# Where the sums over an expert's slots stand in TensorE's order: behind the first half of a gate and up group

## The chip, the cores and the metric

The kernel runs on one core of a Trainium2 chip. The metric is the device time of one execution in microseconds (us). TensorE (PE in the profile) multiplies matrices into PSUM, VectorE (DVE) and ScalarE (ACT) move and combine, SyncE (SP) issues the DMA transfers that bring the weights from HBM to SBUF. Each engine works through its own queue of instructions in order; between engines there are semaphores.

## The reference

Two layers of a trunk over 256 tokens of width 1024. Each layer has a token mixer and a channel mixer; the channel mixer of the second layer is a mixture of eight experts of which each token takes two:

```python
def moe_swiglu(x, router, wg, wu, wd):
    ...
    top_val, top_idx = lax.top_k(logits, TOP_K)
    top_w = jax.nn.softmax(top_val, axis=-1)
    gates = jnp.sum(jax.nn.one_hot(top_idx, N_EXPERTS, dtype=jnp.float32) * top_w[..., None], axis=1)
    out = jnp.zeros((B * S, D), jnp.float32)
    for e in range(N_EXPERTS):
        out = out + gates[:, e:e + 1] * swiglu(xt, wg[e], wu[e], wd[e]).astype(jnp.float32)
```

All is float32. An expert's hidden width is 2816, so each of its three weight matrices has 1024 x 2816 elements.

## The kernel before, in words

The change touches the expert stage alone (`moe`, from about 437 us on in the profiled execution). The tokens of an expert are gathered into slots: 64 always (the main slots) and 32 more (the unit slots) when the expert has over 64 tokens, which is known on the chip only; a flag for each expert is read into a register, and a condition on it chooses at run time. Up to 96 slots are thus computed in one round, and further rounds are skipped unless an expert has more tokens.

An expert is worked through in three chunks of its hidden width (1024, 1024 and 768). For each chunk:

- the gate and up group: 32 products for the main slots (L756, `gu<-raw,xg`, 64 rows out) and 32 for the unit slots, over eight tiles `raw` of weights;
- ScalarE and VectorE make the hidden values from `gu` (L879, L880), and TensorE transposes them into `pt` (L889), which VectorE copies to `hT` (L891);
- the down group of the chunk before (`down`, L756, `y<-raw,hT`), which accumulates over an expert's chunks in two PSUM banks: `y[0]` for the main slots and `y[1]` for the unit slots. `y[1]` is opened and closed by a matmul with zeros (`clear`, L763).

Every group is issued by `in_steps`: first the half of the main products that needs no flag (`ahead`, 16 products, two rows each in the trace), then the condition, then in either branch the rest. A product on TensorE stands in two rows of the trace, as it is float32.

After an expert's last down group, `combine` moves `y` to SBUF as a pair of a rounded part `yh` (ScalarE, L838) and the remainder `yl` (VectorE, L839), six pieces each: two of 64x512 (main slots, from `y[0]`) and four of 32x256 (unit slots, from `y[1]`). `add_up` then sums over the slots: for each of four output quarters a PSUM bank `pc` gets one matmul with `yh` (L848) and one with `yl` (L849), and VectorE adds the bank, times the gate, to `x` (L850). The banks `pc` come from a pool of two, which `pt` shares, so the third pair can be written when the first addition has read its bank. `y` too has a pool of two banks, so the next expert's `y[1]` takes a bank that the expert before has used.

The order on an engine is set by a scheduler that takes what is ready by its place in the program, within the dependences; `behind(a, b)` adds a dependence for the order alone. `flush` calls `add_up` behind the second gate and up group of the next expert; the scheduler drew the sums ahead of that group, since no dependence held them.

The weights pass through a ring of 16 tiles of up to 1 MB: SyncE issues the load of a tile (L744) when TensorE has read what was in it.

Of the kernel before, what the change touches and what calls it, by code (L numbers as in the profile page):

```python
# [54 lines left out]
def hybrid_trunk_kernel(ctx, tc, x_in, w_in, pool_w, relx, w_out, lnrow, vecs, ffn_wg, ffn_wu, ffn_wd,  # L55
                        router, moe_wg, moe_wu, moe_wd, ca_in, cb_in, out):
    nc = tc.nc
# [9 lines left out]
    def bank(pool, tag, name):  # L67
        return pool.tile([P, 512], F32, tag=tag, name=name)
# [41 lines left out]
    def behind(inst, first):  # L110

        tc.add_manual_dep(inst.ins, first.ins.name,
                          mybir.DependencyInfo(mybir.DependencyClass.NoSync, mybir.DependencyReason.DATA),
                          reason="order")
# [508 lines left out]
    def moe(i, mp, pss, r):  # L623
# [5 lines left out]
        yh = mp.tile([P, D], F32R, name="yh")  # L629
# [19 lines left out]
        for t in range(NT):  # L649
# [5 lines left out]
            for hf in range(2):  # L655
                c = slice(hf * 512, (hf + 1) * 512)
                ps = bank(mm, "mm", "xn")
# [51 lines left out]
        def gather(e0, base):  # L709

            pm = mp.tile([P, NT, 2, P], F32R, tag="pm", name="pm")
            pT = mp.tile([P, 2, NT, P], F32R, tag="pmT", name="pmT", bufs=2)
            for j in range(2):
                for t in range(NT):

                    last = nc.vector.tensor_scalar(pm[:, t, j, :], slots, float(base - 4096),
                                                   key[:, t, e0 + j:e0 + j + 1], op0=ALU.add, op1=ALU.is_equal)
            if e0 == 0 and base == 0:
                pm_done.append(last)
                low_parts(last)  # L720
                for t, c, ps in starts:
                    behind(nc.scalar.mul(x[:, t, c], ps, ALPHA), norm)

            g = mp.tile([P, KD, 2 * P], F32, tag="xg", name="xg", bufs=2)
            for k in range(0, KD, 2):
                ps = bank(tr, "tr", "pg")
                for kk in range(2):
                    for n, (src, t) in enumerate((s, t) for s in (nh, nl) for t in range(NT)):
                        nc.tensor.matmul(ps[:, kk * 256:(kk + 1) * 256], src[:, t, (k + kk) * P:(k + kk + 1) * P],
                                         pm[:, t, :, :], start=(n == 0), stop=(n == 2 * NT - 1))  # L730
                nc.scalar.activation(g[:, k:k + 2, :], ps.rearrange("p (a n) -> p a n", a=2), AF.Copy)
            for j in range(2):
                ps = bank(tr, "tr", "pq")
                for t in range(NT):
                    nc.tensor.matmul(ps[:, t * P:(t + 1) * P], pm[:, t, j, :], identr, start=True, stop=True)
                nc.scalar.activation(pT[:, j, :, :], ps[:, :S].rearrange("p (t n) -> p t n", t=NT), AF.Copy)
            return g, pT
# [14 lines left out]
        order = [None]  # L752
# [8 lines left out]
        def clear(ps, n=512, first=True, last=True):  # L761

            nc.tensor.matmul(ps[:, :n], zero[:, :P], zero[:, :n], start=first, stop=last)  # L763

        def in_steps(flag, ahead, main, unit, rest):


            order[0] = None
            if flag is None:
                ahead()  # L770
                main()
                unit(0)
                unit(1)
                return
            ahead()
            with tc.If(flag > 0) as has:
                order[0] = None
                unit(0)
                main()
                unit(1)  # L780
            with has.Else():
                order[0] = None
                rest()
                main()
            order[0] = None

        def experts(base):
# [9 lines left out]
            for e in range(NE):  # L797
                if e == 0:
                    g, pT = gather(e, base)
# [12 lines left out]
                def down(f0, n, hT, e=e, y=y, flag=flag):  # L812

                    nj = n // P
                    wd = moe_wd[e][f0:f0 + n, :].rearrange("(p j) d -> p j d", j=nj)
                    if not y:
                        y.extend(bank(yp, "yp", "y") for _ in range(2))
                        clear(y[1], 256, last=False)
                    ws = [pieces(wd[:, j:j + 2, :], D) for j in range(0, nj, 2)]

                    def part(sls, js, own):
                        for j in js:
                            for sl, b, r, c in sls:
                                product(y[b][r:r + sl.stop - sl.start, :c.stop - c.start], hT[:, j, sl],
                                        ws[j // 2][:, j % 2, c], own and f0 == 0 and j == 0,
                                        own and f0 + n == DFF and j == nj - 1)

                    steps = range(4), range(4, nj)
                    main, unit = blocks(D)[:2], blocks(D)[2:]
                    in_steps(flag, lambda: part(main, steps[0], True), lambda: part(main, steps[1], True),  # L830
                             lambda i: part(unit, steps[i], False), lambda: None)
                    if f0 + n == DFF:
                        clear(y[1], 256, first=False)

                def combine(e=e, pT=pT, y=y):
                    for sl, b, r, c in blocks(D):
                        ps = y[b][r:r + sl.stop - sl.start, :c.stop - c.start]
                        last_yh[0] = nc.scalar.activation(yh[sl, c], ps, AF.Copy)  # L838
                        nc.vector.tensor_sub(yl[sl, c], ps, yh[sl, c])  # L839

                    sums.append(lambda: add_up(e, pT))

                def add_up(e, pT):
                    for hf in range(2):
                        c = slice(hf * 512, (hf + 1) * 512)
                        for t in range(NT):
                            ps = bank(tr, "tr", "pc")
                            nc.tensor.matmul(ps, pT[:, e % 2, t, :], yh[:, c], start=True, stop=False)  # L848
                            nc.tensor.matmul(ps, pT[:, e % 2, t, :], yl[:, c], start=False, stop=True)  # L849
                            nc.vector.scalar_tensor_tensor(x[:, t, c], ps, gate[:, t, e:e + 1], x[:, t, c],  # L850
                                                           op0=ALU.mult, op1=ALU.add)

                for ci, (f0, n) in enumerate(ECH):
# [6 lines left out]
                    def part(m, k0, ws=ws, gu=gu, g=g, w=w):  # L860
                        s0 = 0 if m == MAIN else MAIN

                        for k in (k0 + 2, k0 + 3, k0, k0 + 1):
                            for b in range(2):
                                for i in range(2):
                                    bk, r = (b, i * MAIN) if m == MAIN else (2, (2 * i + b) * UNIT)
                                    product(gu[bk][r:r + m, :w], g[:, k, o + s0:o + s0 + m],
                                            ws[k // 2][1 - i][:, k % 2, b * w:(b + 1) * w], k == 2, k == KD - 3)

                    in_steps(flag, lambda: part(MAIN, 0), lambda: part(MAIN, 4), lambda i: part(UNIT, 4 * i),  # L870
                             lambda: clear(gu[2], w))
                    if e % 2 and e + 1 < NE and ci == len(ECH) - 1:
                        nxt = gather(e + 1, base)
                    s = mp.tile([P, 1024], F32, tag="silu", name="silu", bufs=2)
                    for b in range(2):
                        c = slice(b * w, (b + 1) * w)
# [17 lines left out]
                    if ci == len(ECH) - 1:  # L894
                        later.append(combine)
                        if e % 2 and e + 1 < NE:
                            g, pT = nxt
# [13 lines left out]
        for t in range(NT):  # L911
            mu, r = moments(t)
            for hf in range(2):
                c = slice(hf * 512, (hf + 1) * 512)
# [21 lines left out]
    with tc.tile_pool(name="moe", bufs=1) as mp, tc.tile_pool(name="ring2", bufs=RING2) as ring2:  # L936
        rings.append((ring2, RING2))
        ring_pos[0] = 0
        moe(1, mp, pss, r)
# [56 lines left out]
```

## Time and profile before

| | |
|---|---|
| time, three runs | 1170.47, 1172.53, 1173.04 us (median 1172.53) |
| the profiled execution | 1171.37 us, span of its instructions 1169.6 us |
| TensorE busy | 1112.1 us (95% of the span) |
| VectorE, ScalarE busy | 425.3 us, 292.6 us |
| mean granted TensorE clock | 0.965 of full speed |
| DMA, 450 to 1150 us | 264.23 MB, mean 377 GB/s |

The profile lists for each engine what it did and what ended its waits. [...] A row of the timeline merges equal instructions that follow each other: start, duration to the end of the last, engine, line, operation, names, and in brackets the idle time ahead of it and what ended it.

### The profile page before, as it was taken

To read this page: it belongs to the slowest core of one execution; us is meant where nothing else is said; L and a number is where in the kernel's file an instruction comes from. 1 tells how busy PE (TensorE), PEld (TensorE's weight loads), DVE (VectorE), ACT (ScalarE), POOL (GpSimd) and SP (SyncE) were. 2 spreads that over 40 slices of the span, in tenths; PEclk is the share of its full clock that TensorE was granted. 3 is DMA by queue.
4 is the path that set the end of the run, shared out by engine and by line. 5 is a ranking of instruction groups with operands and counts; after the bars stand their busy time and mean duration, and the time that the engine had idled before them with its cause. 6 is when DMAs were issued, how large, how long until landed. Compare 5 with 4: busy or idle time off the path is not lost. (4 is left out here: it accounts for less than half of the span.)

```text
span 1169.6 us, 15303 instructions
## 1 busy us (share of the span) xinstructions
PE 1112.1 (95%) x6494; PEld 616.6 (53%) x6494; DVE 425.3 (36%) x708; ACT 292.6 (25%) x450; POOL 3.2 (0%) x15
## 2 busy tenths in 40 slices
PE   8999999999999999998998998998998998998995
PEld 6987688888789774333433332433333443333333
DVE  3677755453597763113113113113113112113115
ACT  2455454443345643001101001101001101001001
POOL 0000000000000000000000000000000000000000
PEclk9999999999999988998998998999998999998996
DMA  8942385555276259999999899989899989999911
GB/s 252 315 154 72 122 274 180 180 181 172 79 266 225 73 197 415 408 416 415 411 369 416 344 413 414 414 352 413 342 415 414 411 338 415 356 413 418 413 60 38
DMA packets 108766, 350.19 MB, mean 299 GB/s; under 512 B 7680, under 2 KB 31360, under 8 KB 97408
## 3 DMA queue, kind: packets, MB, share of 16 engines
q1 hardware_dynamic: 108528, 348.75, 77.1%
q8 instruction: 73, 1.20, 0.4%
q14 instruction: 21, 0.17, 0.0%
q10 hardware_dynamic: 144, 0.07, 0.0%
HBM read 347.75 MB, written 1.05 MB: 298 GB/s over the span
## 5 line engine op out<-in xcount | busy, mean ns | idle before, releaser
L756 PE MATMUL gu<-raw,xg 128*64 128x512 f32 (+3 forms) x2304 | 401.6, 568 | 0.5 <-issue 0.5
L756 PEld LDWEIGHTS gu<-raw,xg 128*64 128x64 f32 (+1 forms) x2304 | 131.2, 130 | 252.6 <-issue 248.3
L880 DVE TENSOR_TENSOR silu<-silu,gu 64x512 f32<-64x512 f32 (+1 forms) x96 | 61.9, 645 | 432.1 <-ACT silu L879 429.7
L756 PE MATMUL y<-raw,hT 128*64 128x512 f32 (+1 forms) x1408 | 200.9, 489 | 0.0
L879 ACT ACTIVATE silu<-gu 64x512 f32<-64x512 f32 (+1 forms) x96 | 53.1, 553 | 501.6 <-PE gu L756 496.4
L126 DVE TENSOR_TENSOR lo<-raw,hi 128x2048 fp32r<-128x2048 f32 (+1 forms) x57 | 128.0, 2251 | 84.8 <-ACT hi L125 84.8
L125 ACT ACTIVATE hi<-raw 128x2048 fp32r<-128x2048 f32 (+1 forms) x57 | 107.4, 1883 | 135.1 <-PE gu L146 42.1
L756 PEld LDWEIGHTS y<-raw,hT 128*64 128x64 f32 (+1 forms) x1408 | 68.1, 123 | 121.3 <-issue 107.8
L144 PE MATMUL ps<-xTh,hi 128*128 128x256 f32 x224 | 65.2, 291 | 1.2 <-DVE vs L348 0.7
L146 PE MATMUL ps<-xTh,lo 128*128 128x256 f32 x224 | 64.5, 288 | 1.6 <-DVE lo L126 1.6
L144 PE MATMUL gu<-hi,xTh 128*128 128x512 f32 (+1 forms) x176 | 65.9, 374 | 0.0
L145 PE MATMUL gu<-lo,xTh 128*128 128x512 f32 (+1 forms) x176 | 65.7, 373 | 0.0
L146 PE MATMUL gu<-hi,xTl 128*128 128x512 f32 (+1 forms) x176 | 65.5, 372 | 0.0
L145 PE MATMUL ps<-xTl,hi 128*128 128x256 f32 x224 | 64.4, 287 | 0.0
L891 DVE COPY hT<-pt 128x384 f32<-128x384 f32 (+1 forms) x48 | 22.9, 519 | 94.7 <-PE pt L889 94.7
L144 PEld LDWEIGHTS ps<-xTh,hi 128*128 128x128 f32 x224 | 43.5, 194 | 2.5 <-issue 1.0
L146 PEld LDWEIGHTS ps<-xTh,lo 128*128 128x128 f32 x224 | 43.6, 195 | 2.2 <-DVE lo L126 1.8
L145 PEld LDWEIGHTS ps<-xTl,hi 128*128 128x128 f32 x224 | 43.5, 194 | 0.4 <-issue 0.3
L848 PE MATMUL pc<-yh,pmT 128*128 128x512 f32 x32 | 15.8, 586 | 28.4 <-ACT yh L838 28.4
L838 ACT ACTIVATE yh<-y 32x256 fp32r<-32x256 f32 (+1 forms) x48 | 21.5, 447 | 77.9 <-PE y L756 47.9
L145 PEld LDWEIGHTS gu<-lo,xTh 128*128 128x128 f32 x176 | 33.2, 188 | 5.7 <-DVE lo L126 0.3
L146 PEld LDWEIGHTS gu<-hi,xTl 128*128 128x128 f32 x176 | 33.2, 188 | 5.7 <-issue 0.2
(186 smaller groups left out, 1078.8 us busy)
## 6 DMA issues: line engine op xcount, KB each, us to landing
raw<-in_moe_wd_dram SPq DMA_DIRECT2D x88, 1024.0 KB, 13.1
raw<-in_moe_wu_dram SPq DMA_DIRECT2D x64, 1024.0 KB, 14.0
raw<-in_moe_wg_dram SPq DMA_DIRECT2D x64, 1024.0 KB, 15.2
raw<-in_moe_wu_dram SPq DMA_DIRECT2D x32, 768.0 KB, 12.5
raw<-in_moe_wg_dram SPq DMA_DIRECT2D x32, 768.0 KB, 14.2
raw<-in_w_in_dram SPq DMA_DIRECT2D x14, 1024.0 KB, 9.8
raw<-in_ffn_wg_dram SPq DMA_DIRECT2D x11, 1024.0 KB, 5.1
raw<-in_ffn_wu_dram SPq DMA_DIRECT2D x11, 1024.0 KB, 5.0
```

What stands on the lines that cost most here:

```text
L125: cv = nc.scalar.activation(hi[:, :a * n], raw[:, :a * n], AF.Copy)
L126: ld = nc.vector.tensor_sub(lo[:, :a * n], raw[:, :a * n], hi[:, :a * n])
L144: nc.tensor.matmul(o, ah, bh, start=first, stop=False)
L145: nc.tensor.matmul(o, ah, bl, start=False, stop=False)
L146: nc.tensor.matmul(o, al, bh, start=False, stop=last)
L756: mi = nc.tensor.matmul(o, a, b, start=first, stop=last)
L838: last_yh[0] = nc.scalar.activation(yh[sl, c], ps, AF.Copy)
L848: nc.tensor.matmul(ps, pT[:, e % 2, t, :], yh[:, c], start=True, stop=False)
L879: nc.scalar.activation(s[sl, c], gu[bk][rg:rg + m, :w], AF.Silu)
L880: nc.vector.tensor_mul(s[sl, c], s[sl, c], gu[bk][ru:ru + m, :w])
L891: nc.vector.tensor_copy(hT[:, j0:j0 + m, :], pt[:, :m * SLOTS].rearrange("p (j q) -> p j q", q=SLOTS))
```

## The change: what it does

`in_steps` remembers the last product of the half that stands ahead of the condition, and the first matmul of each of the four pairs of `add_up` gets an order dependence on it. So the sums of expert e are issued behind the 16 products `ahead` of the group that was begun last, and in front of that group's condition.

```diff
+        last_ahead = [None]
+
         def in_steps(flag, ahead, main, unit, rest):
             order[0] = None
             if flag is None:
                 ahead()
+                last_ahead[0] = order[0]
                 main()
                 unit(0)
                 unit(1)
                 return
             ahead()
+            last_ahead[0] = order[0]
             with tc.If(flag > 0) as has:
...
                         for t in range(NT):
                             ps = bank(tr, "tr", "pc")
-                            nc.tensor.matmul(ps, pT[:, e % 2, t, :], yh[:, c], start=True, stop=False)
+                            behind(nc.tensor.matmul(ps, pT[:, e % 2, t, :], yh[:, c], start=True, stop=False),
+                                   last_ahead[0])
                             nc.tensor.matmul(ps, pT[:, e % 2, t, :], yl[:, c], start=False, stop=True)
```

On TensorE, where one expert ends and the next has begun, this stood in a row before, from the matmul that closes the old `y[1]` to the first product of the next group (a name in brackets is the semaphore of the engine or DMA queue that the instruction waits for):

```order
L763 MATMUL y<-zero 128x256
L848 MATMUL pc<-yh,pmT 128x512 [waits Activation_49]
L848 MATMUL pc<-yh,pmT 128x512 [waits DVE_49]
L763 LDWEIGHTS zero
L763 MATMUL y<-zero 128x256 [waits DVE_49]
L849 MATMUL pc<-yl,pmT 128x512 [waits DVE_49]
L849 MATMUL pc<-yl,pmT 128x512
L848 MATMUL pc<-yh,pmT 128x512 [waits Activation_49]
L848 MATMUL pc<-yh,pmT 128x512 [waits DVE_49]
L849 MATMUL pc<-yl,pmT 128x512 [waits DVE_49]
L849 MATMUL pc<-yl,pmT 128x512
L756 MATMUL gu<-raw,xg 64x512 [waits DMAHW2_49]
```

And this stands there now, from the matmul that opens the next expert's `y[1]` on; "..." stands for the rest of the 16 products (a line number that is 4 or 5 higher is the same statement):

```order
L763 LDWEIGHTS zero
L763 MATMUL y<-zero 128x256 [waits DVE_49]
L756 MATMUL gu<-raw,xg 64x512 [waits DMAHW2_49,Activation_49]
...
L852 MATMUL pc<-yh,pmT 128x512 [waits PE_49,Activation_49]
L854 MATMUL pc<-yl,pmT 128x512 [waits DVE_49]
L852 MATMUL pc<-yh,pmT 128x512 [waits PE_49]
L854 MATMUL pc<-yl,pmT 128x512
L852 MATMUL pc<-yh,pmT 128x512 [waits DVE_49,Activation_49]
L854 MATMUL pc<-yl,pmT 128x512
L852 MATMUL pc<-yh,pmT 128x512 [waits DVE_49]
L854 MATMUL pc<-yl,pmT 128x512
L780 COMPARE_AND_BRANCH
```

The eight matmuls of the sums have gone from ahead of the 16 products to behind them, directly ahead of the condition; the second matmul with zeros, which opens the next `y[1]` and waits for VectorE, has stayed where it was and now stands directly ahead of the products. The count of VectorE that it waits for is in the built program, in both kernels and at all seven places, that of the third piece of `yl` (the second of 64x512). This holds at the seven changes from one expert to the next; behind the last expert nothing moves.

On VectorE, between the copies of `hT` and the next group's hidden values, this stood before:

```order
L839 TENSOR_TENSOR yl<-y,yh 64x512
L839 TENSOR_TENSOR yl<-y,yh 32x256
L839 TENSOR_TENSOR yl<-y,yh 64x512
L839 TENSOR_TENSOR yl<-y,yh 32x256
L850 SCALAR_TENSOR_TENSOR x<-pc,gate,x 128x512
L839 TENSOR_TENSOR yl<-y,yh 32x256
L850 SCALAR_TENSOR_TENSOR x<-pc,gate,x 128x512
L839 TENSOR_TENSOR yl<-y,yh 32x256
L850 SCALAR_TENSOR_TENSOR x<-pc,gate,x 128x512 x2
```

And now:

```order
L843 TENSOR_TENSOR yl<-y,yh 64x512
L843 TENSOR_TENSOR yl<-y,yh 32x256
L843 TENSOR_TENSOR yl<-y,yh 64x512
L843 TENSOR_TENSOR yl<-y,yh 32x256 x3
L855 SCALAR_TENSOR_TENSOR x<-pc,gate,x 128x512 x4
```

The last two pieces of `yl` no longer stand behind additions that wait for the sums. ScalarE, GpSimd and SyncE have the same order in both kernels.

## Rows read from the trace of the kernel before

**Rows 1.** The page: busy us, share of the span, instructions

```profile
PE 1112.1 (95%) x6494; PEld 616.6 (53%) x6494; DVE 425.3 (36%) x708; ACT 292.6 (25%) x450; POOL 3.2 (0%) x15
```

**Rows 2.** Who waited for whom, 450 to 1150 us: total us, times, longest

```profile
PE pc L848 <- ACT yh L838: 27.0, 15, 2.3
...
PEld gu L756 <- DMA raw<-in_moe_wd_dram: 2.1, 5, 0.7
```

**Rows 3.** What the DMA queue of SyncE waited for, 450 to 1150 us

```profile
SPq L744 <- PE gu L756: 168.6, 45, 13.6
```

**Rows 4.** DMA, 450 to 1150 us: GB/s in 40 slices, total

```profile
GB/s 419 402 416 419 409 420 406 362 397 413 415 294 415 413 418 413 416 374 347 412 415 292 413 418 411 418 409 415 285 410 422 317 412 414 411 424 402 417 14 1
DMA packets 61460, 264.23 MB, mean 377 GB/s; under 512 B 4287, under 2 KB 4287, under 8 KB 50135
```

**Rows 5.** Timeline of TensorE at the first change of expert, 528 to 552 us

```profile
534.44 0.28 PE L763 MATMUL y<-zero 1*128 1x256 bf16 x1
536.92 0.74 PE L848 MATMUL pc<-yh,pmT 128*128 128x512 f32 x2 [2.20 <-ACT yh L838]
537.59 0.39 PE L763 MATMUL y<-zero 1*128 1x256 bf16 x1
537.91 1.22 PE L849 MATMUL pc<-yl,pmT 128*128 128x512 f32 x2
540.41 1.22 PE L848 MATMUL pc<-yh,pmT 128*128 128x512 f32 x2 [1.28 <-ACT yh L838]
541.43 1.05 PE L849 MATMUL pc<-yl,pmT 128*128 128x512 f32 x2
542.41 9.88 PE L756 MATMUL gu<-raw,xg 128*64 128x512 f32 x48
```

**Rows 6.** Timeline of VectorE at the same place

```profile
536.50 1.14 DVE L839 TENSOR_TENSOR yl<-y,yh 64x512 fp32r<-64x512 f32 x2 [0.21 <-ACT yh L838]
538.74 0.75 DVE L850 SCALAR_TENSOR_TENSOR x<-pc,gate,x 128x512 f32<-128x512 f32 x1 [1.10 <-PE pc L849]
539.52 0.42 DVE L839 TENSOR_TENSOR yl<-y,yh 32x256 fp32r<-32x256 f32 x1
```

**Rows 7.** Timeline of ScalarE at the same place

```profile
535.87 0.99 ACT L838 ACTIVATE yh<-y 64x512 fp32r<-64x512 f32 x2 [0.74 <-DVE yl L839]
```

**Rows 8.** Groups by line and form, 450 to 1150 us: busy us, mean ns

```profile
L850 DVE SCALAR_TENSOR_TENSOR x<-pc,gate,x 128x512 f32<-128x512 f32 x32 | 23.3, 748 | 14.4 <-PE pc L849 14.2
...
L839 DVE TENSOR_TENSOR yl<-y,yh 64x512 fp32r<-64x512 f32 x16 | 11.0, 688 | 17.7 <-ACT yh L838 17.5
```

**Rows 9.** Stretches of 2 us there: length, busy PE, PEld, DVE, ACT, POOL, clock, DMA

```profile
535.00:537.00 2.00, 0.08 (x1) 0.08 (x1) 1.72 (x4) 1.10 (x3) 0.00 (x0) 1.00 1.01 408
537.00:539.00 2.00, 2.00 (x5) 0.81 (x5) 0.87 (x3) 0.38 (x1) 0.00 (x0) 0.63 1.03 424
...
543.00:545.00 2.00, 2.00 (x8) 0.60 (x6) 0.50 (x1) 0.00 (x0) 0.00 (x0) 0.67 1.03 430
```

**Rows 10.** Stretches, seven changes of expert: first matmul with zeros ended, `ahead` ended

```profile
534.72:550.43 15.71, 12.23 (x46) 4.50 (x49) 6.38 (x11) 2.09 (x5) 0.00 (x0) 0.78 1.02 424
...
1066.05:1082.13 16.08, 12.42 (x45) 4.42 (x49) 6.37 (x11) 2.09 (x5) 0.00 (x0) 0.79 1.02 422
sum 110.87, PE 86.20 PEld 31.01 DVE 44.60 ACT 14.64 POOL 0.00; mean PE 12.31 PEld 4.43 DVE 6.37 ACT 2.09 POOL 0.00
```

**Rows 11.** Timeline of TensorE in expert 0: 16 products in a row

```profile
455.68 7.09 PE L756 MATMUL gu<-raw,xg 128*64 128x512 f32 x32
```

**Rows 12.** Stretches of 1 us early in the program, columns as in rows 9

```profile
37.00:38.00 1.00, 0.00 (x0) 0.00 (x0) 1.00 (x1) 1.00 (x1) 0.00 (x0) 1.00 1.09 386
...
39.00:40.00 1.00, 1.00 (x7) 1.00 (x7) 0.94 (x3) 0.55 (x1) 0.00 (x0) 0.58 1.01 344
...
42.00:43.00 1.00, 1.00 (x8) 1.00 (x8) 1.00 (x1) 0.21 (x1) 0.00 (x0) 0.71 1.05 375
```

**Rows 13.** TensorE's sequencer at the conditions: ns min/median/max, first and last start

```profile
L776 PEldq COMPARE_BRANCH  x72: 65/174/1977, 450.1 to 1143.7; - x72
```

## The prediction

> **What bounds the kernel now.** I read the page first: TensorE is busy for 1112.1 us of a span of 1169.6 us [rows 1]. Then who waited for whom in the expert stage. TensorE itself waits for almost nothing there but ScalarE's `yh` ahead of the sums, 27.0 us in 15 waits; for the weights only its weight loads wait, and the longest such total is 2.1 us in 5 waits [rows 2]. The transfers, on the other side, wait for TensorE to free tiles of the ring: 168.6 us at its gate and up products alone [rows 3]. At their best they run at some 415 GB/s, over the stage at 377 [rows 4], so 264.23 MB need at least 264.23 / 0.415 = 637 us of 700, and there are 63 us of slack. So TensorE is the bound, and time saved on it at a change of expert should reach the end.
>
> The timeline of TensorE at one change of expert shows what is to be had [rows 5]. The first matmul with zeros ends at 534.72. TensorE is idle for 2.20 us until `yh` is there, does two matmuls of the sums, opens the next `y[1]`, does two more, is idle for another 1.28 us, does the last four, and begins the 16 products at 542.41. The second idle stretch comes from VectorE's order: a piece of `yl` starts only at 539.52, behind an addition that had waited for the sums [rows 6].
>
> The clock is the second thing to see. It is at the upper level in the first idle stretch, and 0.63 on the mean from 537 to 539, so it fell at 537 + 2 x (1 - 0.37 / 0.5) = 537.5; 0.67 from 543 to 545 puts its rise at 544.3 [rows 9]. That is 6.8 us at the lower level, with an idle stretch inside it and the 16 products only at its end. All seven changes look alike: 15.71 to 16.08 us from the end of the first matmul with zeros to the end of the 16 products, 110.87 us in all (15.84 each), and a mean clock of 0.78 or 0.79, which over 15.8 us is 6.6 to 7.0 us at the lower level [rows 10].
>
> **The change part by part.** No instruction is added and none taken away; the eight matmuls of the sums move behind the 16 products at seven places. I rebuild the same interval with the new order.
>
> 1. The wait that stays. The matmul that opens the next `y[1]` now stands ahead of the products, and TensorE takes its matmuls in order. It needs the third piece of `yl`: VectorE starts that at 536.50 [rows 6] and takes 0.69 us [rows 8], so 537.19. From ScalarE's end at 535.87 + 0.99 = 536.86 [rows 7] to the matmul that it released at 536.92 [rows 5] it is 0.06 us; the same here gives 537.25. TensorE is thus idle for 537.25 - 534.72 = 2.53 us, where it was idle for 2.20. Nothing on VectorE or ScalarE ahead of that piece moves, so I take it as fixed.
> 2. The matmul with zeros, to the start of what follows: 537.59 to 537.91, 0.3 us [rows 5].
> 3. The 16 products: 7.09 us at the upper level [rows 11]. Their weights were landed long before; beginning them some 5 us earlier needs no transfer that TensorE waits for in the rows.
> 4. The lower level. The wait of 2.53 us is longer than the one behind which the clock fell seven times, so I let it fall again. How long it stays low is nowhere shown for this order, so I bound it: nothing if it does not fall; 6.8 us as now; or what an early place shows. There TensorE was idle (busy 0.00 from 37 to 38), the clock was 0.58 on the mean of 39 to 40 and 0.71 of 42 to 43, so it was low from 39.16 to 42.58, 3.4 us, with TensorE busy without a break [rows 12]. Behind the wait there now stand 7 us of products without a break, so I take this row: 3.4 us at half speed cost 1.7 us. The ends are 0 and 3.4 us.
> 5. The sums, at the upper level. The pairs `yh`, `yl` for the third and fourth bank wait for the first and second addition, as there are two banks. At the upper level the first two matmuls start 0.34 us apart (0.67 us to the next row for two [rows 5]). From the start of a `yl` matmul to its addition it is 0.83 us at the lower level (537.91 to 538.74 [rows 5, 6]), about 0.5 at the upper; two additions take 2 x 0.75 [rows 8]; the last pair starts 0.06 later and takes 2 x 0.34. So 0.34 + 0.5 + 1.5 + 0.06 + 0.68 = 3.1 us at most. The other end is eight matmuls at half of the 0.51 us between their starts at the lower level (541.43 - 540.41 for two [rows 5]), 2.0 us. The chain of additions is the nearer, but part of the 0.68 is generous: 2.8 us. All of `yh` and `yl` is ready long before, behind 7 us of products, and so costs nothing; without that cover it would be the 1.28 us of now.
> 6. The condition now stands behind matmuls that wait, with only the last pair in TensorE's queue to cover it. Its median is 0.17 us [rows 13], inside the 0.34 us of one matmul: nothing, up to 1.98 - 0.34 = 1.6 us at its longest.
>
> The interval becomes 2.53 + 0.3 + 7.09 + 1.7 + 2.8 = 14.4 us, 1.4 less than 15.84; seven times, 9.9 us. What follows is unchanged in order. VectorE's additions come later, but nothing reads `x` before the end, and the banks that they free are next wanted by transposes behind a whole group. SyncE gets the tiles of the 16 products back earlier, which helps the transfers. Behind the last expert nothing changes.
>
> The profiled execution took 1171.37 us around its span of 1169.6, so 1161.5; the median of the three runs is 1.16 us above it, so I predict 1162.6 us.
>
> [...]
>
> **The rivals.**
>
> - The lower level lasts as long as now. For it: seven of seven stretches were 6.8 us. Against it: in each of them there was an idle stretch of 1.28 us or more inside, which is gone, and the early row is 3.4 us. Price: 1.7 us more at each place, 16.1 us against 15.84, so 2.0 us slower than before, 1174.5; with the sums at 3.1 us, 4.1 slower, 1176.6. It decides where item 4 costs over 3.1 us. Slower or no change.
> - The condition is exposed at its longest each time: 7 x 1.6 = 11.5 us, so 1174.1, slower by 1.6. It decides from 1.4 us each. The median of 0.17 speaks against it, and where the expert has unit slots the code goes straight on.
> - The clock does not fall, or falls late, since the work behind the wait is dense: 7 x 1.7 = 12 us less, 1150.6. Against it: seven falls of seven behind a shorter wait.
> - The transfers take back half, because TensorE gains on them in a stretch: 1167.5. For it: weight loads did wait 2.1 us in 5 places [rows 2], and slices with gaps lie beside full ones at 415 GB/s [rows 4]. Against it: 63 us of slack, and tiles freed earlier.
>
> **How the numbers follow.** Chances: the forecast 0.63; the clock's stretch as long as now 0.13 (0.08 of it within 0.2% and 0.05 slower); the condition 0.04; no fall 0.10; the transfers 0.08; 0.02 for something else that is slower. A measurement of this kernel tells about 0.2% (2.3 us) from no change. Faster: 0.63 + 0.10 + 0.08 = 0.81, taken as 0.80; within 0.2%: 0.08 and most of the condition's, 0.12; slower: 0.08. The forecast's own range is 1157 to 1167: the sums at 2.0 us give 5.6 us more, at 3.1 us 2.1 less, and a place or two with a long stretch 1.7 each. The range for 8 in 10 leaves out the rival without a fall (0.10) and the slower ones beyond the nearest (0.08): 1155 to 1175.
>
> **What would show it.** Per step: an idle stretch of about 2.5 us ahead of the second matmul with zeros, released by VectorE's `yl`; the 16 products directly behind it, in 8.8 us instead of 7.09; a low clock of 3.4 us at each of seven places; then eight matmuls of the sums in 2 to 3.1 us with a short wait for additions; a mean interval near 14.4 us; a mean clock of the run some 0.01 higher than 0.965. Wrong would be: a clock at 0.50 for nearly 7 us into the products, a gap between the sums and what follows the condition, waits of TensorE for weights above the few us of now, or no idle stretch ahead of the products.

## The result, and the profile after

The change makes the kernel faster: 1159.89 us (median of four runs, 1159.42 to 1160.76) against 1172.78 us (four runs of the kernel before beside them, 1170.47 to 1173.22), a ratio of 0.9895 with an interval of 0.9881 to 0.9909. The profiled execution took 1159.93 us, its span is 1158.1 us, the mean granted clock 0.973 instead of 0.965.

The page, busy time of the engines and the clock in 40 slices ("answers [rows 1]" means: the same view as there, now of the changed kernel or of the one under test):

```profile
PE 1105.2 (95%) x6494; PEld 612.8 (53%) x6494; DVE 424.6 (37%) x708; ACT 292.3 (25%) x450; POOL 3.2 (0%) x15
...
PEclk9999999999999988999999999999999999999996
```

TensorE is busy for 6.9 us less, with the same 6494 instructions: the same matmuls at a higher clock, 0.973 on the mean against 0.965. At the seven changes of expert, whose stretches follow below, it is 86.20 - 80.29 = 5.9 us of busy time less; the other 3.7 us saved there are idle time.

The timeline of TensorE at the first change of expert (answers [rows 5]):

```profile
532.52 0.28 PE L763 MATMUL y<-zero 1*128 1x256 bf16 x1
535.32 0.26 PE L763 MATMUL y<-zero 1*128 1x256 bf16 x1 [2.52 <-DVE yl L843]
535.51 8.78 PE L756 MATMUL gu<-raw,xg 128*64 128x512 f32 x32
544.22 0.51 PE L852 MATMUL pc<-yh,pmT 128*128 128x512 f32 x1
544.57 0.40 PE L854 MATMUL pc<-yl,pmT 128*128 128x512 f32 x1
...
545.90 0.47 PE L852 MATMUL pc<-yh,pmT 128*128 128x512 f32 x1 [0.47 <-DVE x L855]
...
546.47 0.51 PE L852 MATMUL pc<-yh,pmT 128*128 128x512 f32 x1
546.81 0.40 PE L854 MATMUL pc<-yl,pmT 128*128 128x512 f32 x1
547.14 5.08 PE L756 MATMUL gu<-raw,xg 128*32 128x512 f32 x38
```

The first idle stretch has grown from 2.20 to 2.52 us, and its releaser is another one: VectorE's `yl`, for which the opening of the next `y[1]` waits. The second idle stretch, 1.28 us, is gone; 0.47 us of waiting for an addition is what the sums have of their own. Behind the last `yl` matmul the unit products follow at once, so the condition between them shows no gap.

The timeline of VectorE there (answers [rows 6]):

```profile
533.23 1.13 DVE L843 TENSOR_TENSOR yl<-y,yh 64x512 fp32r<-64x512 f32 x2
534.57 1.14 DVE L843 TENSOR_TENSOR yl<-y,yh 64x512 fp32r<-64x512 f32 x2 [0.21 <-ACT yh L842]
...
545.00 1.41 DVE L855 SCALAR_TENSOR_TENSOR x<-pc,gate,x 128x512 f32<-128x512 f32 x2 [7.56 <-PE pc L854]
546.65 1.41 DVE L855 SCALAR_TENSOR_TENSOR x<-pc,gate,x 128x512 f32<-128x512 f32 x2 [0.23 <-PE pc L854]
```

In its second row, a piece of 64x512 and one of 32x256 in one, lies the third piece of `yl`; TensorE's wait ends at 535.32, as that piece ends. The additions now start 7.56 us behind the last piece of `yl`, and nothing waits for them but the third pair of the sums.

The seven intervals from the end of the first matmul with zeros to the end of the later of `ahead` and the sums, so over the same work as [rows 10]:

```profile
532.80:547.21 14.41, 11.43 (x45) 3.93 (x48) 5.43 (x10) 2.09 (x5) 0.00 (x0) 0.88 1.03 425
630.69:646.09 15.40, 12.40 (x42) 4.15 (x41) 5.43 (x10) 2.09 (x5) 0.00 (x0) 0.78 0.84 334
...
sum 101.24, PE 80.29 PEld 27.66 DVE 37.98 ACT 14.61 POOL 0.00; mean PE 11.47 PEld 3.95 DVE 5.43 ACT 2.09 POOL 0.00
```

101.24 against 110.87 us are 9.6 us saved at the seven places. Six of them take 14.20 to 14.41 us at a clock of 0.88; the second takes 15.40 at 0.78. The clock in stretches of 2 us at the first and at the second change (answers [rows 9]):

```profile
535.00:537.00 2.00, 1.68 (x7) 0.58 (x8) 1.10 (x3) 0.75 (x2) 0.00 (x0) 0.84 1.02 420
537.00:539.00 2.00, 2.00 (x6) 0.48 (x4) 0.43 (x1) 0.00 (x0) 0.00 (x0) 0.50 1.04 428
539.00:541.00 2.00, 2.00 (x10) 0.67 (x8) 0.00 (x0) 0.00 (x0) 0.00 (x0) 0.81 1.03 420
...
631.00:633.00 2.00, 0.00 (x0) 0.00 (x0) 1.73 (x4) 1.12 (x3) 0.00 (x0) 0.73 0.98 406
...
637.00:639.00 2.00, 2.00 (x8) 0.64 (x6) 0.00 (x0) 0.00 (x0) 0.00 (x0) 0.56 1.03 402
```

Read as in the prediction: 0.84 puts the fall at 537 - 2 x (1 - 0.84) / 0.5 = 536.36, 0.81 the rise at 539.76, so 3.4 us at the lower level, the 0.50 that the stretch between them shows. It is the level of the kernel before too, in a stretch that lies wholly between the fall at 537.5 and the rise at 544.3:

```profile
539.00:541.00 2.00, 0.72 (x2) 0.51 (x2) 1.91 (x4) 0.38 (x1) 0.00 (x0) 0.50 1.05 430
```

The clock fell 1.04 us after the wait had ended (535.32), when TensorE was at work again. At the second change 0.73 puts the fall at 631.92, in the middle of the idle stretch, and 0.56 the rise at 638.76: 6.8 us. The timeline there shows what it costs, 9.68 us for the 16 products instead of 8.78:

```profile
633.21 0.37 PE L763 MATMUL y<-zero 1*128 1x256 bf16 x1 [2.52 <-DVE yl L843]
633.51 9.68 PE L756 MATMUL gu<-raw,xg 128*64 128x512 f32 x32
```

What TensorE waited for from 440 to 1140 us (answers [rows 2]; total us, times, longest):

```profile
PE y L763 <- DVE yl L843: 17.7, 7, 2.5
PE pc L852 <- ACT yh L842: 3.8, 2, 2.3
PE pc L852 <- DVE x L855: 3.3, 7, 0.5
...
PE gu L756 <- issue: 0.4, 1, 0.4
```

Its sequencer at the conditions (answers [rows 13]):

```profile
L780 PEldq COMPARE_BRANCH  x72: 65/176/1971, 448.2 to 1132.1; - x72
```

Of the 27.0 us for `yh`, 2.3 lay behind the last expert; the other 24.7, at the seven places, have become 17.7 us for `yl` and 3.3 for the additions. The 3.8 us for `yh` that are left stand behind the last expert. The conditions take what they took, and none of the seven behind the sums is followed by a wait of TensorE: the one idle stretch ahead of gate and up products, the last line above, lies at 461.26 us.

The profiled executions differ by 1171.37 - 1159.93 = 11.4 us, 1.8 more than the seven places give. The first gather's row shows why:

```profile
436.58 0.80 PE L729 MATMUL pg<-pm,nh 128*128 128x256 f32 x2
```

In the kernel before the same matmuls began at 439.12, though nothing ahead of them differs. Over all the kernels profiled here that start lies anywhere from 436.57 to 439.85 us, with no relation to what was changed behind it. From there to the end of the span it is 1169.6 - 439.12 = 730.5 us before and 721.5 after, 9.0 us less.

### The profile page after: what moved, and what is told of

The parts are those of the page before. It is cut to its first block, busy times and chain, and to the rows that moved or that the text cites. A ratio compares the mean times of both kernels' runs of the same rounds, so it can differ in the third digit from the quotient of the medians.

```text
span 1158.1 us, 15324 instructions
## 1 busy us (share of the span) xinstructions
PE 1105.2 (95%) x6494; PEld 612.8 (53%) x6494; DVE 424.6 (37%) x708; ACT 292.3 (25%) x450; POOL 3.2 (0%) x15
## 5 line engine op out<-in xcount | busy, mean ns | idle before, releaser
L855 DVE SCALAR_TENSOR_TENSOR x<-pc,gate,x 128x512 f32<-128x512 f32 x32 | 22.6, 747 | 56.5 <-PE pc L854 56.4
```

## The experiments

The theory: the sums had stood in front of the products with a wait ahead of them and one inside; behind the products they find everything ready, and the clock, which falls behind the wait that stays, comes back after 3.4 us instead of 6.8, since no idle stretch follows. The rivals that the result leaves: VectorE's new order is what helps; the condition or the transfers take part of it back; and, beside them, the question what the wait that stays still costs. All ratios are to the kernel before on the same chip.

**The changed kernel once more**, for its spread.

> The changed kernel again, to size the gain. Rows of the two profiled executions give 9.6 us over the seven changes of expert (110.87 against 101.24 us), the medians 12.9. My theory (one wait of 2.5 us stays at each place, the lower clock stretch halves from 6.8 to 3.4 us, and the second idle stretch is gone): 10 to 13 us faster than before, about 1160 us, with a stretch of 6.8 us only where the clock falls well before the wait has ended. Rival (part of the difference is luck of one execution's clock early in the program): 8 us or less.

Measured: 1160.68 us (six runs, 1159.81 to 1163.93) against 1171.86, 0.9914 (0.9894 to 0.9934). In its profiled execution all seven low stretches are 3.4 us, the clock falling from 0.17 us ahead of the end of the wait to 1.48 us after it, and from the first gather to the end it is 1158.7 - 438.36 = 720.3 us. So the gain is 11 to 13 us by medians and 9 to 10 by the stage's own length.

**VectorE's order alone**: the sums stay in front, but the additions stand behind the last piece of `yl`.

```diff
-                        nc.vector.tensor_sub(yl[sl, c], ps, yh[sl, c])
+                        last_yl[0] = nc.vector.tensor_sub(yl[sl, c], ps, yh[sl, c])
...
-                            nc.vector.scalar_tensor_tensor(x[:, t, c], ps, gate[:, t, e:e + 1], x[:, t, c],
-                                                           op0=ALU.mult, op1=ALU.add)
+                            add = nc.vector.scalar_tensor_tensor(x[:, t, c], ps, gate[:, t, e:e + 1], x[:, t, c],
+                                                                 op0=ALU.mult, op1=ALU.add)
+                            if e + 1 < NE:
+                                behind(add, last_yl[0])
```

> The kernel before, with VectorE's additions behind the last piece of yl, as the change put them; the sums stay ahead of the products. Rival (the gain came from VectorE's order, which took the second idle stretch away): as fast as the changed kernel, 1160 us. My theory (it came from work without waits behind the one wait): the third pair of the sums still waits for an addition, which now starts later, so an idle stretch of 1 us or more stays in the lower clock stretch, which stays at 6.8 us; 0 to 5 us faster than before, 1168 to 1173 us.

Measured: 1171.41 us (12 runs, 1169.90 to 1172.57), 0.9996 (0.9985 to 1.0006): no change. The timeline of TensorE in that kernel:

```profile
534.79 0.28 PE L763 MATMUL y<-zero 1*128 1x256 bf16 x1
537.27 0.73 PE L848 MATMUL pc<-yh,pmT 128*128 128x512 f32 x2 [2.20 <-ACT yh L838]
...
540.66 0.76 PE L848 MATMUL pc<-yh,pmT 128*128 128x512 f32 x1 [1.70 <-DVE x L850]
...
542.63 9.90 PE L756 MATMUL gu<-raw,xg 128*64 128x512 f32 x44
```

The second idle stretch has only changed its releaser: from `yh`, 1.28 us, to the addition that must free a bank of `pc`, 1.70 us. From the end of the first matmul with zeros to the products it is 542.63 - 535.07 = 7.56 us, against 7.69 in [rows 5]. VectorE's order alone is not the cause of the gain.

**The opening of `y[1]` behind the products too.** The changed kernel keeps a wait of 2.52 us, for a matmul with zeros; the first product into the bank that it opens starts at 565.43, 30 us later.

```diff
-            nc.tensor.matmul(ps[:, :n], zero[:, :P], zero[:, :n], start=first, stop=last)
+            return nc.tensor.matmul(ps[:, :n], zero[:, :P], zero[:, :n], start=first, stop=last)
...
-                        clear(y[1], 256, last=False)
+                        opened = clear(y[1], 256, last=False)
+                        if e:
+                            behind(opened, last_ahead[0])
```

> The changed kernel, with the matmul with zeros that opens the next expert's y[1] behind the 16 products too. My theory: nothing waits ahead of the products, no idle stretch of 2.5 us, no fall of the clock at the seven places; the interval is 7.1 + 0.3 + 2.9 = 10.3 us against 14.4, so 7 x 4.1 = 29 us faster than the changed kernel, about 1131 us. Rival (the transfers bind once TensorE is that much faster): TensorE's weight loads wait some us for transfers at several places and half or less of the 29 us is seen, 1145 us or more. Second rival (the clock falls whatever stands there): about 1143 us.

Measured: 1138.76 us (five runs, 1138.01 to 1142.48), 0.9722 (0.9701 to 0.9742): 21.9 us faster than the changed one on the same chip, and between the theory's 1131 us and the rival's 1145. The timeline of TensorE at the first change:

```profile
535.61 0.28 PE L763 MATMUL y<-zero 1*128 1x256 bf16 x1
535.82 7.09 PE L756 MATMUL gu<-raw,xg 128*64 128x512 f32 x32
542.83 0.51 PE L854 MATMUL pc<-yh,pmT 128*128 128x512 f32 x1
...
543.98 0.28 PE L763 MATMUL y<-zero 1*128 1x256 bf16 x1
544.51 0.47 PE L854 MATMUL pc<-yh,pmT 128*128 128x512 f32 x1 [0.26 <-DVE x L857]
```

And what TensorE waited for longest from 440 to 1140 us:

```profile
PE gu L756 <- DMA raw<-in_moe_wg_dram: 7.4, 3, 3.2
```

No idle stretch at the change, no fall of the clock: the products take their 7.09 us, as in [rows 11], and the opening lies in the pause that the sums have anyway. All seven intervals (cut as those above) are 9.91 or 9.92 us, less than the 10.3 expected, so the time lacking to 1131 us lies elsewhere. The last line shows where: TensorE now waits for weights, 7.4 us in three places, and behind one of these waits the clock falls too (0.50 from 1014 to 1016 us). The profiled execution took 1142.48 us and is the slowest of the five, so the others may have waited less. The DMA view of this kernel from 440 to 1130 us shows the cause (answers [rows 4]):

```profile
GB/s 407 405 409 416 414 413 413 413 413 414 420 405 419 408 419 418 407 418 407 416 414 414 411 420 410 418 409 391 403 409 422 403 418 414 414 417 410 310 1 4
```

The slices with gaps, seven below 375 GB/s in [rows 4] ahead of the last two, are gone until the weights run out: the transfers have become the bound.

**The same two kernels with fewer loads.** The last weight tile of each down group is not loaded, and the group's first tile stands in for it: 24 of 280 loads less, and no matmul less.

```diff
-                    ws = [pieces(wd[:, j:j + 2, :], D) for j in range(0, nj, 2)]
+                    ws = [pieces(wd[:, j:j + 2, :], D) for j in range(0, nj - 2, 2)]
+                    ws.append(ws[0])
```

> The kernel with the opening matmul behind the products too, and with the last of each down group's weight tiles not loaded but the group's first tile used again (24 of 280 loads fewer; the down products of those rows use wrong weights). Theory (what that kernel lacked of its 29 us were waits for transfers, some 8.4 us of idle time ahead of gate and up products and one fall of the clock): those waits are gone, 1131 us. Rival (it lacked them for another reason, in the order): no faster than it was, 1139 us.

> The changed kernel with the same loads left out (the last tile of each down group is the group's first again). Theory (the changed kernel's TensorE waits for no transfers): the same as the changed kernel, 1160 us. Rival (transfers already take back some of the gain): faster by more than 3 us.

Measured with the opening behind the products: 1127.45 us (five runs, 1126.09 to 1130.34), 0.9625 (0.9609 to 0.9640); with the opening ahead, as in the changed kernel: 1159.67 (four runs, 1158.99 to 1162.32), 0.9902 (0.9885 to 0.9920). Fewer loads give the changed kernel nothing that these runs can tell, so the transfers took nothing back from the change. They give the kernel with the late opening what it lacked, and 3.5 us more than the 1131 expected; TensorE's products wait for weights no more, and the first interval, cut as those above, is

```profile
533.12:543.03 9.91, 9.65 (x45) 3.56 (x49) 5.42 (x10) 2.09 (x5) 0.00 (x0) 1.00 1.01 418
```

9.91 against 14.41 us: 4.5 us is what the wait that stayed costs the changed kernel at this place. All seven intervals here add up to 69.49 us, against 101.24, so it is 31.8 us in seven; 1159.67 - 1127.45 = 32.2 us is what the two medians say. The terms of the 4.5: 2.52 us of idling, 1.7 of a low clock behind it, and 0.2 to 0.3 for a matmul that has a free place inside the sums.

**The opening alone behind the products**, the sums left in front as before (the edit of the late opening, put into the kernel before, with the two lines of `in_steps` that remember the last of the products).

> The kernel before, with only the opening matmul moved behind the 16 products; the sums stay ahead of them. Theory (there the opening matmul never waited, as the sums beside it wait longer): no change, 1171 to 1173 us. Rival (moving it shortens the waits by itself): 4 us faster or more.

Measured: 1172.14 us (11 runs, 1167.80 to 1172.95), 0.9993 (0.9982 to 1.0004): no change.

```profile
534.95 0.74 PE L854 MATMUL pc<-yh,pmT 128*128 128x512 f32 x2 [2.19 <-ACT yh L844]
...
537.94 1.22 PE L854 MATMUL pc<-yh,pmT 128*128 128x512 f32 x2 [1.43 <-ACT yh L844]
...
539.94 8.64 PE L756 MATMUL gu<-raw,xg 128*64 128x512 f32 x32
```

The sums wait at the same place, 2.19 and 1.43 us, and the clock is low for 6.8 us at all seven changes. So the move of the opening is worth nothing by itself, the move of the sums 11 us by itself, and both together 33.

**A shorter wait.** The changed kernel, with VectorE's copies of `hT` at the change of expert put behind the second large piece of `yl`.

```diff
-                        nc.vector.tensor_sub(yl[sl, c], ps, yh[sl, c])
+                        mi = nc.vector.tensor_sub(yl[sl, c], ps, yh[sl, c])
+                        if b == 0:
+                            large_yl[0] = mi
...
-                        nc.vector.tensor_copy(hT[:, j0:j0 + m, :],
-                                              pt[:, :m * SLOTS].rearrange("p (j q) -> p j q", q=SLOTS))
+                        cp = nc.vector.tensor_copy(hT[:, j0:j0 + m, :],
+                                                   pt[:, :m * SLOTS].rearrange("p (j q) -> p j q", q=SLOTS))
+                        if e and ci == 0:
+                            behind(cp, large_yl[0])
```

> The changed kernel, with VectorE's two copies of hT behind the second large piece of yl instead of ahead of the first. My theory: that piece is ready some 0.7 us earlier, so the wait is 1.8 us instead of 2.52, 5 us over the seven places: about 1155 us with the clock falling as now. If the clock falls at fewer places behind a shorter wait, up to 1.7 us more at each, down to 1143 us. Rival (the wait is set by ScalarE's pieces and not by these copies): no change, 1160 us.

Measured: 1152.18 us (six runs, 1145.54 to 1154.11), 0.9823 (0.9795 to 0.9851), 8.5 us faster than the changed kernel on the same chip. The timeline at the first and at the third change:

```profile
535.56 0.26 PE L763 MATMUL y<-zero 1*128 1x256 bf16 x1 [1.81 <-DVE yl L843]
535.76 7.09 PE L756 MATMUL gu<-raw,xg 128*64 128x512 f32 x32
...
705.21 0.36 PE L763 MATMUL y<-zero 1*128 1x256 bf16 x1 [1.86 <-DVE yl L843]
```

The clock at the third, in stretches of 2 us:

```profile
703.00:705.00 2.00, 0.34 (x3) 0.11 (x2) 1.44 (x3) 1.34 (x3) 0.00 (x0) 0.91 1.02 410
...
711.00:713.00 2.00, 2.00 (x10) 0.56 (x8) 0.00 (x0) 0.00 (x0) 0.00 (x0) 0.89 1.02 422
```

TensorE's wait is 13.0 us in seven places instead of 17.7, 4.7 less. The clock adds to that: it fell at four places only, twice for 6.8 us (at the third from 704.64 to 711.44, the first 0.57 us of it idle) and twice for 3.4; at the other three the products took 7.09 us. These four stretches are 20.4 us, some 1.2 of it idle, and cost half of the rest, 9.6; the seven of 3.4 us in the changed kernel run once more cost 11.8. That is 2.2 less, 6.9 together, and from the first gather to the end it is 1150.1 - 437.51 = 712.6 us, 7.7 less than there. The runs of this kernel lie 8.6 us apart, more than those of any other.

**The sums in the middle of the products**: behind 8 of the 16, so that eight products stand between them and the condition.

```diff
-                            nc.tensor.matmul(ps, pT[:, e % 2, t, :], yl[:, c], start=False, stop=True)
+                            mi = nc.tensor.matmul(ps, pT[:, e % 2, t, :], yl[:, c], start=False, stop=True)
...
+                    return mi
...
                         for k in (k0 + 2, k0 + 3, k0, k0 + 1):
+                            if m == MAIN and k0 == 0 and k == 0 and sums:
+                                last_ahead[0] = order[0]
+                                while sums:
+                                    order[0] = sums.pop(0)()
```

> The changed kernel, with the sums behind 8 of the 16 products and the other 8 behind the sums, so that 8 products again stand between the sums and the condition. Rival (the condition directly behind the sums costs time): faster than the changed kernel by what it cost, 0.3 to 1.6 us at each of seven places, 2 to 11 us. My theory (the condition is hidden, and yh and yl are ready within the first 2 us of the products): the same as the changed kernel, 1160 us within 2 us.

Measured: 1164.11 us (six runs, 1159.77 to 1165.54), 0.9925 (0.9907 to 0.9944). The timeline of TensorE in that kernel:

```profile
538.30 0.26 PE L763 MATMUL y<-zero 1*128 1x256 bf16 x1 [2.53 <-DVE yl L843]
538.50 5.35 PE L756 MATMUL gu<-raw,xg 128*64 128x512 f32 x16
543.78 0.50 PE L852 MATMUL pc<-yh,pmT 128*128 128x512 f32 x1
...
546.68 5.51 PE L756 MATMUL gu<-raw,xg 128*64 128x512 f32 x32
```

With eight products, some 3.5 us by half of [rows 11], between the sums and the condition it is not faster, as the rival would have it; together with the missing waits behind the conditions above, this shows no loss there. The expectation of 1160 us within 2 us was missed, by 4.1 us, but its interval and that of the changed kernel run once more (0.9894 to 0.9934) overlap. In its profiled execution the clock fell at six places, at three of them for 6.8 us; from the first gather to the end it is 722.7 us, against 719.6 to 721.5 in the three of the changed order.

## Why the prediction was right, step by step

The time of 1159.89 us lies within the forecast's own range of 1157 to 1167, 2.7 us below the value, and the ratio in its two measurements, 0.9895 and 0.9914, is near the 1162.6 / 1172.53 = 0.9915 that was predicted.

- Item 1, the wait that stays: 2.52 us for 2.53, released by VectorE's third piece of `yl`, at all seven places (17.7 us in 7).
- Item 2, the matmul with zeros: the products begin 0.19 us behind its start, not 0.3.
- Items 3 and 4, the products and the clock: 544.22 - 535.51 = 8.71 us for 8.79. The clock fell at all seven places and was low for 3.4 us at six of them. Without the fall the products take 7.09 us, as the kernel with the late opening shows. The early stretch of [rows 12] gave the right length, and the half speed that the prediction counts with is the 0.50 of the stretches above.
- Item 5, the sums: 547.21 - 544.22 = 2.99 us for 2.8; the chain of two additions was the right bound, and its upper value of 3.1 the better guess.
- Item 6, the condition: no gap in the rows, and eight products in front of it bring nothing. The conditions at the seven places take 0.07 us at the four where the unit products follow and 0.22 to 0.33 us at the other three; the longest of all 72, 1.97 us, is again the exception beside a median of 0.18, and the 1174.1 us of the rival with an exposed condition did not come.

The interval of a short stretch is thus 2.52 + 0.19 + 8.71 + 2.99 = 14.41 us for 14.4. That it comes so close is partly luck, since items 2 and 5 missed by 0.1 and 0.2 us in opposite directions. The sum over seven was 9.6 us by the rows for 9.9: the six places with a short stretch saved 1.5 us each for 1.4, the second, with its long one, 0.3 (15.40 for 15.69, which is the shortest of the seven before, where the prediction reads 15.71).

Of the rivals, **the lower level as long as now** came at one place of seven here, at none in the second profile of this kernel and at two with fewer loads. The reason given against it, that there is no second idle stretch, holds: the kernel before and the two that keep the sums in front, each with a second stretch of idling, have 6.8 us at 21 places of 21. But it is not the whole of it. In the five profiles that keep the wait and have no second one (this kernel twice, with fewer loads, with the shorter wait, with the sums in the middle), the long stretches, eight, are those in which the clock fell 0.52 to 1.29 us before the wait ended; in the 22 short ones it fell at most 0.38 us before that, or after. Which of the two it is goes with where the fall lies against the wait. That moved from run to run and is not in the prediction, so that six of seven were short is partly luck: with the sums in the middle it was three of six. The price of this rival was too high as well: 1.7 us more at each place were forecast, and the three long stretches of the changed order and of the one with fewer loads took 15.40, 15.50 and 15.63 us, 1.0 to 1.2 more than a short one, since part of the low clock then lies in the wait. Even at 15.6 everywhere the kernel would not be slower than before. **No fall of the clock** was the exception while the wait was 2.5 us (2 of 28 places in four profiles); it took a shorter wait (3 of 7 at 1.81 to 1.86 us) or none.

**The transfers** were rightly taken as covered, but by a slack that was too large. The prediction had 63 us, all of the stage against the best rate. The last two slices of [rows 4] carry 14 and 1 GB/s; there is nothing left to load in them, and 2 x 17.5 us = 35 us of the 63 lie there. That leaves 28 us, enough for a gain of 10, not for the 31.8 us more of the late opening, which is where the waits for weights appeared.

The medians give 11 to 13 us where the stage's own length gives 9 to 10, but the latter rests on one profile of the kernel before, 730.5 us. The two kernels that were no faster than it, with VectorE's order alone and with the opening alone, take 731.9 and 731.8 us from the first gather to the end, and measured against these the changed kernel in its two profiles gains 10 to 12. What is left of the difference stays open; the start of the first gather alone differs by up to 3.3 us between profiled executions. Open is also whether the sums in the middle cost the 1 to 4 us by which they seem slower, or only met more early falls of the clock, and what sets the moment of a fall.

## What to carry to other kernels

When work that waits is moved behind work that is ready, look at what else in that engine's queue waits for the same source: here one matmul with zeros, for a bank that is first used 30 us later, kept the idle stretch where it was and cost 4.5 us at each of seven places. A wait on TensorE was paid a second time here by the low clock behind it, 1.7 us for one of 2.5: taking 17.7 us of waits away gave 32.2 us, and shortening them by 4.7 gave 8.5. And two moves of which one gains 11 us and the other nothing can gain 33 together. Slack of the transfers is to be counted only up to the last load, here 28 us and not 63.

## What the runs showed of the hardware

- At the changes of expert, with the one wait left in, TensorE's clock was at its lower level, 0.50, for 3.4 or for 6.8 us and for nothing in between, 22 and 8 times of 35 in five profiles; 5 times it did not fall at all. The moment of the fall, against the end of the wait, ranged from 1.29 us before to 1.48 us after.
- At idle stretches of 1.81 to 1.86 us, in them or behind them, it fell at 4 places of 7, at those of 2.52 us at 26 of 28.
- In the kernel with the late opening the transfers held 391 to 422 GB/s, slice by slice, for 37 slices of 17.25 us; the gaps of [rows 4], down to 285 GB/s, were waits for tiles (168.6 us at the gate and up products, [rows 3]) and not a limit of the transfers.
